# A one-core hybrid layer (SSD, attention, hierarchical MoE): the overflow loop moves from behind the last expert group into the first one

## The chip, the cores and the metric

One NeuronCore of a Trainium2 chip runs the whole program. The metric is the device time of one execution in microseconds (us): 540.91 us is the median of three runs of the kernel before (540.25 to 541.68). Engines are named as in the profile: PE (TensorE matmul) with PEld (its weight loads), DVE (VectorE), ACT (ScalarE), POOL (GpSimd) and SP (SyncE, which here issues all weight loads).

## The reference

```
h   = RMSNorm(x)                          # x: 256 rows of 1024, float32
[z | xBC | dt | q | k | v | g_ssd | g_att] = h @ W_in
y_s = Mamba-2 SSD(z, xBC, dt) @ W_ssd_out
y_a = MoBA(rope(q), rope(k), v) @ W_att_out
x   = x + (sigmoid(g_ssd) * y_s + sigmoid(g_att) * y_a) @ W_o
x   = x + HierMoE(RMSNorm(x))             # top 1 of 4 groups, in it top 2 of 8 experts
gate = sigmoid(RMSNorm(x) @ W_pg)
x   = x + gate * (p @ W_ple)
out = RMSNorm(x)
```

HierMoE is, for each expert e that a row chose, `(silu(x @ w_gate[e]) * (x @ w_up[e])) @ w_down[e]` times the row's weight for e. There are 32 experts with three matrices of 1 MiB each (1024x256, 1024x256 and 256x1024 float32). 256 rows make 512 choices.

## The kernel before

**Stages.** In-projection, SSD, attention and the output projections fill the first 297 us. A middle part of the program then normalizes the new x (in the tile `x_sb`), forms the router's logits (`plg`), chooses experts and ranks the choices of each expert (`choose`, `rank`, `select`, `combine`), and gathers rows for the first experts. The expert stage follows, then a tail: transposes of the sum `y_sb` (`x3_T`), the split of it into a high and a low part (`x3_out`: ACT writes `x3_hi`, DVE `x3_lo`), the same split of the gate matrix W_pg (`gate_hi` on ACT, `gate_lo` on DVE), 3-pass matmuls of both (`ple_gate`), and the last RMSNorm.

**Expert stage.** The function `quad(q)` handles experts 4q to 4q+3. Each expert has 32 slots, so that the four fill 128 rows. The rows are gathered by matmuls with a one-hot matrix (`gat`, evicted into `hTg`); the gate phase multiplies them with the four gate matrices (`gu<-wg`), the up phase with the up matrices (`gu<-wu`), 64 matmul instructions each, as 8 steps of k times 4 experts. `hidden` applies the nonlinearity and transposes (`hq`), `down` makes `py` in two column halves of 512, `ye` is its copy, and `sca` scatters it back to the 256 rows, where DVE adds it into `y_sb`. The group q = 7 is the last: its halves of `py` are scattered each as soon as it is there.

**Overflow.** An expert that was chosen by more than 32 rows has choices left over. `count_rounds` computes how many further rounds that takes (`nov`), and `overflow_rounds` is a loop with that count at run time, `tc.For_i(0, nov, 1)`, which handles up to 8 expert-with-32-slots pieces a round. In the executions here nov is 0: no instruction of the loop's body is in the trace. The loop stands behind the last group, ahead of the tail.

**Order of the loads.** All weights come by SP, one load of 1 MiB into one of 26 pages (8 KB on each of 128 partitions), in the order of the list `queue`: four gate matrices, four up matrices, four down matrices for each group. A load is issued when `prefetch(n)` is reached in the program and a page and one of 8 semaphores of the DMA queue are free; so at most 8 loads are under way. `NPRE = 25` expert loads are asked for ahead of the expert stage, and each phase of a group asks for as many as pages it gave back. The last four down matrices come in halves (`d0`, `d1`), and behind them two of the four pages of W_pg (`pgr`); the other two are asked for behind the loop.

**Order on the engines.** PE, ACT, DVE and POOL follow the written order inside blocks of `manual_schedule` (the middle part and the tail are such blocks) and an order that a scheduler finds elsewhere (the groups 0 to 6). SP always follows the written order. All engines meet at the loop.

Of the kernel before, what the change touches and what calls it, by code (L numbers as in the profile page):

```python
# [15 lines left out]
OP = mybir.AluOpType  # L16
# [166 lines left out]
def emit(ctx, tc, nc, A, out):  # L183
# [8 lines left out]
    def pg(shape, name, dt=F32):  # L192
        return pgp.tile([P] + shape, dt, tag="pg", name=name)
# [622 lines left out]
    def expert_load(e, w):  # L816
        if w[0] == "d":
            if w != "d1":
                EW["d", e] = pg([4, 512], f"wd{e}")
            r = slice(2 * int(w[1]), 2 * int(w[1]) + 2) if w[1:] else slice(0, 4)  # L820
            SP.dma_start(EW["d", e][:, r], A["w_d"][e].rearrange("(p r) d -> p r d", r=4)[:, r])
        else:
            t = pg([NK, 256], f"w{w}{e}")
            SP.dma_start(t, A["w_" + w][e].rearrange("(p k) f -> p k f", k=NK))
            EW[w, e] = t

# [20 lines left out]
    queue = deque((expert_load, 4 * q + j, w) for q in range(NE // 4) for w in "gud" for j in range(4))  # L847
    for _ in range(4):
# [245 lines left out]
    def count_rounds():  # L1094

        pc = ps3([1], "ocount", parts=NE)
        for t in range(NT):
            mm(pc, mk[:, t, :], onesb[:, 0:1], t == 0, t == NT - 1)
        cnt, more, total = tn([1], "ocn0")[0:NE], tn([8], "omore", BF16, 1)[0:NE], tn([1], "ototal", F32, 1)[0:1]
        V.tensor_copy(cnt, pc)  # L1100
        yield
        V.tensor_scalar(more, C("r32")[0:NE], cnt, None, op0=OP.is_lt)
        yield
        pm = ps3([8], "omorep", parts=1)
        mm(pm, onesb[0:NE, 0:1], more, True, True)
        for _ in range(4):
            yield
# [17 lines left out]

    def gather_mm(pgts, t, rhs):
        for k in range(NK):
            mm(pgts[k // 4][:, k % 4, :], x_sb[:, t, k * P:(k + 1) * P], rhs, t + k % 4 == 0, t == NT - 1)
# [66 lines left out]
    middle.__exit__(None, None, None)  # L1195
    for _ in count_rounds():
        pass
    pgts = psos = wrw = None
# [27 lines left out]

    def hidden(pgu, f, n, name, filler=lambda: None):
        hq = qt([512], "hq" + name)
# [4 lines left out]
        filler()  # L1233
        pt = ps2([2, n], "hdT" + name)
# [43 lines left out]

    def quad(q, filler=lambda: None):
        if q:  # L1280
# [6 lines left out]
        for i, w in enumerate("gu"):  # L1287
            if (q, i) == (7, 1):
                sw, f = combine_weights(q, sel)
            for js in GU_ORDER.get((q, i), ((0, 1, 2, 3),)):  # L1290
                for k in range(NK):
                    for j in js:
                        mm(pgu[32 * j:32 * j + 32, 256 * i:256 * i + 256], g(k)[:, 32 * j:32 * j + 32],
                           EW[w, 4 * q + j][:, k, :], k == 0, k == NK - 1)
                for j in js:
                    EW.pop((w, 4 * q + j))
# [6 lines left out]
        hT = hidden(pgu, f, P, str(q), filler)  # L1303
        if q == 7:
# [9 lines left out]
    def overflow_rounds():  # L1314

        nov = nc.values_load(nov_i, min_val=0, max_val=MAXOV - 1,
                             skip_runtime_bounds_check_because="512 choices fill at most 15 rounds beyond the first")
        with tc.For_i(0, nov, 1) as it:
            work = qt([512], "owork")
            pc = ps2([1], "ocnt", parts=NE)  # L1320
# [53 lines left out]
            g = ow = None  # L1374
            sw = weights_T(work[:, 192:192 + NT * CAP], work[:, 256:512], CAP, "o")
            f = factors(lambda t: so[:, t], CAP, "o")
            hT = hidden(pgu, f, CAP, "o")
            for n in range(2):
                s = slice(512 * n, 512 * n + 512)
                py = ps1([512], f"pyo{n}", parts=CAP)  # L1380
                for c in range(2):
# [3 lines left out]
                ow = None  # L1385
                y = qt([512], f"yo{n}")
                SC.copy(y[0:CAP], py)
# [156 lines left out]
    hT = None  # L1544
    gate_hi(0, 0, range(4))
    end.__exit__(None, None, None)
    sw = y = None
# [3 lines left out]
    end.__enter__()  # L1551
# [4 lines left out]
    x3_out(*d10)
# [62 lines left out]
```

## Time and profile before

| | us |
|---|---|
| median of 3 runs | 540.91 (540.25 to 541.68) |
| the profiled execution, its own time | 538.34 |
| its span in the trace | 536.6 |
| PE busy | 497.5 (93%) |
| DVE busy | 287.9 (54%) |
| ACT busy | 212.5 (40%) |
| DMA | 154.77 MB, mean 288 GB/s over the span |

The profiled execution took 1.74 us more than its span and 2.57 us less than the median. Times below are on the axis of that trace (us from the span's start). A chain of waits follows the work that ended last back from the last instruction. A window row gives the busy time of each engine in a stretch, the granted PE clock as a share of 2.4 GHz, the busy share of the DMA engines and what they moved. On DMA rows the landing is the time from the issue by SP to the last byte.

### The profile page before, as it was taken

What the parts mean: (1) busy time and instruction counts of PE and PEld (TensorE: products, weight loads), DVE (VectorE), ACT (ScalarE), POOL (GpSimd) and SP (SyncE); (2) the same over time, 40 slices, a digit from 0 to 9 for tenths busy, and PEclk for the clock granted to TensorE, in tenths of its full rate; (3) what the DMA queues carried; (4) which work ended last, traced back from release to release, by engine and by line L of the source; (5) the groups of instructions that cost most, each with busy time, mean ns of one, the idle gap of its engine ahead of it and who ended that gap; (6) DMA issues with size and microseconds to landing.
All of it is one profiled execution on the core that took longest, in us unless ns stands there. A gap on an engine that the chain in (4) does not pass through costs nothing. (4 is left out here: it accounts for less than half of the span.)

```text
span 536.6 us, 9525 instructions
## 1 busy us (share of the span) xinstructions
PE 497.5 (93%) x3911; PEld 382.6 (71%) x3911; DVE 287.9 (54%) x586; ACT 212.5 (40%) x427; POOL 16.0 (3%) x22
## 2 busy tenths in 40 slices
PE   6999999999999999999999999889898899887793
PEld 3899888798899979999988746355363536352583
DVE  5899788878477595745583612313133220121675
ACT  5927759518375095532352311111111112111473
POOL 3000012000000000000000000000000000000001
PEclk9999999999999999999999989899898999999897
DMA  8990087564627224796689999999999999999402
GB/s 310 426 396 2 1 280 279 165 228 161 233 86 308 79 72 164 288 385 263 257 324 408 360 372 421 419 421 423 417 420 420 415 422 421 418 417 402 177 0 78
DMA packets 29264, 154.77 MB, mean 288 GB/s; under 512 B 4242, under 2 KB 9122, under 8 KB 13348
## 3 DMA queue, kind: packets, MB, share of 16 engines
q1 hardware_dynamic: 29220, 154.16, 72.1%
q8 instruction: 31, 0.51, 0.4%
q14 instruction: 13, 0.11, 0.1%
HBM read 153.08 MB, written 1.06 MB: 287 GB/s over the span
## 5 line engine op out<-in xcount | busy, mean ns | idle before, releaser
L295 DVE TENSOR_TENSOR wl<-wr,wh 128x1024 fp32r<-128x1024 f32 (+4 forms) x92 | 100.8, 1132 | 9.5 <-ACT wh L294 8.6
L294 ACT CAST wh<-wr 128x1024 fp32r<-128x1024 f32 (+4 forms) x92 | 82.6, 961 | 14.5 <-DMA wr<-in_w_ao 4.2
L210 PE MATMUL py<-wd,hq 128*32 128x512 f32 x256 | 37.7, 712 | 3.7 <-ACT hq L1238 3.7
L210 PE MATMUL ps_t<-wl,hT_hi 128*128 128x448 f32 (+2 forms) x112 | 39.9, 373 | 1.2 <-DVE wl L295 1.1
L210 PE MATMUL ps_t<-wh,hT_hi 128*128 128x448 f32 (+2 forms) x112 | 39.6, 375 | 0.0
L210 PE MATMUL ps_t<-wh,hT_lo 128*128 128x448 f32 (+2 forms) x112 | 39.0, 366 | 0.0
L210 PE MATMUL gu<-wu,hTg 128*32 128x256 f32 x512 | 33.0, 379 | 1.8 <-DMA wu<-in_w_u 1.8
L1231 DVE SCALAR_TENSOR_TENSOR hq<-hq,gu 128x256 f32<-128x256 f32 x8 | 3.4, 421 | 55.8 <-ACT hq L1230 55.8
L210 PE MATMUL sca<-ye,selw 128*128 128x512 f32 x64 | 30.2, 612 | 1.5 <-DVE ye L1540 0.8
L210 PE MATMUL gat<-sel,x_sb 128*128 128x128 f32 x256 | 30.3, 276 | 0.5 <-DVE sel L1114 0.5
L210 PEld LDWEIGHTS gat<-sel,x_sb 128*128 128x128 f32 x256 | 29.4, 192 | 1.1 <-DVE sel L1114 0.6
L210 PE MATMUL gu<-wg,hTg 128*32 128x256 f32 x512 | 30.1, 381 | 0.0
L210 PEld LDWEIGHTS py<-wd,hq 128*32 128x32 f32 x256 | 10.2, 126 | 25.6 <-issue 19.2
L210 PEld LDWEIGHTS gu<-wu,hTg 128*32 128x32 f32 x512 | 18.1, 110 | 14.5 <-DMA wu<-in_w_u 2.3
L1311 DVE COPY ye<-py 128x512 f32<-128x512 f32 x7 | 4.8, 692 | 40.3 <-PE py L210 40.3
L210 PEld LDWEIGHTS sca<-ye,selw 128*128 128x128 f32 x64 | 10.9, 189 | 20.4 <-issue 9.1
L210 PEld LDWEIGHTS ps_t<-wl,hT_hi 128*128 128x128 f32 x112 | 21.0, 190 | 4.9 <-DVE wl L295 3.3
L1230 ACT ACTIVATE hq<-gu,f 128x256 f32<-128x256 f32 x8 | 3.8, 474 | 47.7 <-PE gu L210 47.5
L210 PEld LDWEIGHTS ps_t<-wh,hT_lo 128*128 128x128 f32 x112 | 21.3, 190 | 1.9 <-DVE hT_lo L360 0.4
L210 PEld LDWEIGHTS gu<-wg,hTg 128*32 128x32 f32 x512 | 15.4, 110 | 9.9
L210 PEld LDWEIGHTS ps_t<-wh,hT_hi 128*128 128x128 f32 x112 | 21.1, 191 | 1.7
L1137 ACT ACTIVATE hTg<-gat,par 128x128 f32<-128x128 f32 x32 | 9.3, 369 | 27.6 <-PE gat L210 26.2
(310 smaller groups left out, 1100.0 us busy)
## 6 DMA issues: line engine op xcount, KB each, us to landing
wg<-in_w_g SPq DMA_DIRECT2D x32, 1024.0 KB, 13.7
wu<-in_w_u SPq DMA_DIRECT2D x32, 1024.0 KB, 17.4
wd<-in_w_d SPq DMA_DIRECT2D x28, 1024.0 KB, 19.8
wr<-in_w_in SPq DMA_DIRECT2D x16, 1024.0 KB, 5.2
wr<-in_w_in SPq DMA_DIRECT2D x10, 896.0 KB, 10.8
wr<-in_w_so SPq DMA_DIRECT2D x4, 1024.0 KB, 4.7
wr<-in_w_ao SPq DMA_DIRECT2D x4, 1024.0 KB, 7.1
wr<-in_w_o SPq DMA_DIRECT2D x4, 1024.0 KB, 6.9
```

The lines of the kernel that those rows point to most:

```text
L210: mm = lambda o, l, r, start, stop: PE.matmul(o, l, r, start=start, stop=stop, skip_group_check=True)
L294: SC.copy(hi[:, s], raw[:, s])
L295: V.tensor_tensor(lo[:, s], raw[:, s], hi[:, s].bitcast(F32), op=OP.subtract)
L1137: SC.activation(dst(k + i, k + i + 1)[:, 0], o[:, i], AF.Copy, scale=R("mnw")[:, k + i:k + i + 1])
L1230: SC.activation(hd[0:n], pgu[:, 0:256], AF.Tanh, scale=f[0:n, 0:1])
L1231: V.scalar_tensor_tensor(hd[0:n], hd[0:n], 1.0, pgu[:, 0:256], op0=OP.add, op1=OP.mult)
L1311: (V.tensor_copy if c else SC.copy)(y[c], py[c])
```

## The change

The loop with its count is moved; the loads at the end are cut and ordered in another way; the tail is written in another order. `overflow_rounds` gets a page of its own in place of small tiles, and `NPRE` is one less.

```diff
-NPRE = 25
+NPRE = 24
-GU_ORDER = {(7, 1): ((0, 1, 2), (3,))}
...
-    queue.extend((expert_load, NE - 4 + j, w) for w in ("d0", "d1") for j in range(4))
+    queue.extend((expert_load, NE - 4 + j, w) for w in ("u0", "u1", "d0", "d1") for j in range(4))
-    queue.extend((ple_gate_load, kh, c) for kh, c in PG_ORDER[:2])
+    queue.extend((ple_gate_load, kh, c) for kh, c in PG_ORDER)
...
-    gather_mm(pgts, 1, flat(sel, 1))
+    count = count_rounds()
+    next(count), next(count)
+    gather_mm(pgts, 1, flat(sel, 1), range(4))
+    next(count)
+    gather_mm(pgts, 1, flat(sel, 1), range(4, 8))
+    weave(count)
     weave(combine(0))
...
     middle.__exit__(None, None, None)
-    for _ in count_rounds():
-        pass
...
+    def first_sums():
+        ys.append(pg([NT, D], "y_sb"))
+        for t in range(NT):
+            SC.copy(ys[0][:, t], x_sb[:, t])
+
     def scatter(sw, y, n, name):
-        before = ys[0] if ys else x_sb
-        if not ys:
-            ys.append(pg([NT, D], "y_sb"))
...
-                V.tensor_tensor(ys[0][:, t, s], before[:, t, s], po, op=OP.add)
+                V.tensor_tensor(ys[0][:, t, s], ys[0][:, t, s], po, op=OP.add)
...
-                prefetch(len(js) - (q == 0))
+            for j in range(4):
+                EW.pop((w, 4 * q + j))
+            if (q, i) == (0, 0):
+                first_sums()
+                overflow_rounds()
+                prefetch(4)
+            else:
+                prefetch(4 - (q == 0))
...
-    for c in range(2):
-        down(7, c, py, hT)
-        (V.tensor_copy if c else SC.copy)(y[c], py[c])
-        for t in range(NT):
-            scatter7(t, c)
-            add7(t, c)
-    gate_hi(0, 0, range(4))
-    end.__exit__(None, None, None)
-    overflow_rounds()
-    ple_gate_load(*PG_ORDER[2]), ple_gate_load(*PG_ORDER[3])
-    end = tc.manual_schedule(engines={ET.PE, ET.Activation, ET.DVE, ET.Pool})
+    def y7(c):
+        SC.copy(y[c][:, 0:256], py[c][:, 0:256])
+        V.tensor_copy(y[c][:, 256:512], py[c][:, 256:512])
+
+    down(7, 0, py, hT)
+    y7(0)
+    for t in range(NT):
+        scatter7(t, 0)
+        add7(t, 0)
+    down(7, 1, py, hT)
     d00 = x3_T(0, 0)
     d10 = x3_T(1, 0)
+    y7(1)
     x3_out(*d00)
+    gate_hi(0, 0, (0, 1))
+    for t in range(NT):
+        scatter7(t, 1)
+    x3_out(*d10)
+    gate_hi(0, 0, (2, 3))
     gate_lo(0, 0, (0, 1))
-    x3_out(*d10)
+    for t in range(NT):
+        add7(t, 1)
     gate_lo(0, 0, (2, 3))
```

**First place: the first group, PE and SP.** The names: `wu3` is an up matrix, `swT0` the transposed combine weights, `pf` a factor, `nov` the loop's count; before, on PE, from the end of the up phase of group 0:

```order
L210 MATMUL gu0_3245<-wu2_2414,hTg01_3179 32x256
L210 MATMUL gu0_3245<-wu3_2416,hTg01_3179 32x256
L1245 MATMUL swT0_3325<-ident_79,selw0_3322 128x128 x2
L210 MATMUL pf0_3329<-fac_2968,sel0_3145 128x2 x2
L210 MATMUL pf1_3500<-fac_2968,sel1_3386 128x2 x2
```

and now:

```order
L209 MATMUL gu0_3243<-wu2_2414,hTg01_3179 32x256
L209 MATMUL gu0_3243<-wu3_2416,hTg01_3179 32x256
L1324 TENSOR_LOAD nov_2969
L1327 COMPARE_AND_BRANCH
L1327 UNCONDITIONAL_BRANCH x2
```

On PE the loop has come to stand behind the whole up phase of group 0 and ahead of its `swT0`, `pf` and `hdT`. On SP, in the list of loads, before:

```order
L821 DMA wd6_3226<-in_w_d 128x2048
L821 DMA wd7_3228<-in_w_d 128x2048
L824 DMA wg8_3230<-in_w_g 128x2048
L824 DMA wg9_3278<-in_w_g 128x2048
L824 DMA wg10_3280<-in_w_g 128x2048
```

and now (the body of the loop is left out):

```order
L820 DMA wd6_3238<-in_w_d 128x2048
L820 DMA wd7_3240<-in_w_d 128x2048
L1324 TENSOR_LOAD nov_2969
L1327 COMPARE_AND_BRANCH
L1327 UNCONDITIONAL_BRANCH x2
...
L825 DMA wg8_3436<-in_w_g 128x2048
L825 DMA wg9_3438<-in_w_g 128x2048
```

The load of wg8, which was the last of the 25 asked for ahead of the expert stage, and every load after it now stand behind the loop in SP's list.

**Second place: the middle part, ACT and DVE.** `sqm` is the sum of squares of x, `xmTs` the evicted transpose for the logits; on ACT now:

```order
L1005 ACTIVATE sqm11_3096,ssm1_2971<-x_sb_76 128x256
L1012 COPY xmTs14_3111<-xmT14_3108 128x256
L1257 COPY y_sb_3276<-x_sb_76 128x1024
L1005 ACTIVATE sqm12_3120,ssm1_2971<-x_sb_76 128x256
L1257 COPY y_sb_3276<-x_sb_76 128x1024
L1012 COPY xmTs16_3129<-xmT16_3126 128x256
```

The two copies of L1257 are new, and ahead of the last transposes; the other four rows stand in this order before as well. On DVE, in front of and in the chain that makes the expert weights (`ng0` is its first instruction; `omore` and `ototal` belong to the count), before:

```order
L1114 TENSOR_TENSOR sel0_3145<-rk1_2967,cst_74 128x128
L1067 TENSOR_SCALAR ng0_3188<-g80_3066 128x1
L1069 TENSOR_TENSOR dd0_3190<-e80_3073 128x1
L1074 TENSOR_TENSOR el0_3070<-mk_2965,oh10_3099 128x32
...
L1134 TENSOR_TENSOR hTg01_3179<-gat0_1_3164,par_75 128x256
...
L1108 TENSOR_REDUCE ototal_3238<-omorep_3241 1x1
```

and now:

```order
L1113 TENSOR_TENSOR sel1_3545<-rk1_2967,cst_74 128x128
L1102 TENSOR_SCALAR omore_3184<-cst_74,ocn0_3183 32x8
L1107 TENSOR_REDUCE ototal_3185<-omorep_3192 1x1
L1109 CAST nov_2969<-ototal_3185 1x1
L1067 TENSOR_SCALAR ng0_3200<-g80_3066 128x1
```

`ototal` and the cast to `nov`, which stood behind the eviction `hTg01`, have moved ahead of `ng0`; `ototal` reads `omorep`, a matmul that PE now has between the two halves of the gather `gat` of row tile 1.

**Third place: the tail, DVE.** `pgl00` is the low part of the first page of W_pg, `sca7..` what the scatter of the last group makes; before, from the first `x3_lo` on:

```order
L1445 TENSOR_TENSOR x3_lo_4427<-x3T00_4747,x3_hi_4426 128x4x128
L1461 SCALAR_TENSOR_TENSOR pgl00_4574<-pgr00_4366,par_75,pgh00_4573 128x512 x2
L1445 TENSOR_TENSOR x3_lo_4427<-x3T10_4752,x3_hi_4426 128x4x128
L1461 SCALAR_TENSOR_TENSOR pgl00_4574<-pgr00_4366,par_75,pgh00_4573 128x512 x2
L1461 SCALAR_TENSOR_TENSOR pgl01_4766<-pgr01_4406,par_75,pgh01_4765 128x512 x2
```

and now:

```order
L1549 COPY ye71_4709<-py7_1_4707 128x256
L1453 TENSOR_TENSOR x3_lo_4594<-x3T00_4734,x3_hi_4593 128x4x128
L1453 TENSOR_TENSOR x3_lo_4594<-x3T10_4739,x3_hi_4593 128x4x128
L1469 SCALAR_TENSOR_TENSOR pgl00_4749<-pgr00_4567,par_75,pgh00_4748 128x512 x2
L1439 TENSOR_TENSOR y_sb_3276<-y_sb_3276,sca701_0_4752 128x512
L1439 TENSOR_TENSOR y_sb_3276<-y_sb_3276,sca711_0_4754 128x512
L1469 SCALAR_TENSOR_TENSOR pgl00_4749<-pgr00_4567,par_75,pgh00_4748 128x512 x2
```

The last two adds into `y_sb` have moved from ahead of the first `x3_lo` to between the halves of `pgl00`.

## Rows read from the trace of the kernel before

**Rows 1.** Windows of 20 us in the expert stage: busy time (and count) of PE, PEld, DVE, ACT, POOL, then the granted PE clock, the DMA share and GB/s.

```profile
320.00:340.00 20.00, 18.05 (x196) 10.44 (x192) 6.00 (x13) 2.36 (x7) 0.00 (x0) 0.99 1.01 422
...
460.00:480.00 20.00, 17.28 (x171) 9.88 (x160) 5.60 (x11) 2.95 (x8) 0.00 (x0) 1.00 1.01 419
```

**Rows 2.** Timeline of PE, ACT and DVE at the end of the expert stage, up to the loop and the first transposes behind it: start, length, engine, line, instruction, count, and in brackets the idle time before it and what ended it.

```profile
481.29 6.26 PE L210 MATMUL gu<-wu,hTg 128*32 128x256 f32 x60 [1.80 <-DMA wu<-in_w_u]
...
487.63 0.47 ACT L1230 ACTIVATE hq<-gu,f 128x256 f32<-128x256 f32 x1 [8.58 <-PE gu L210]
...
490.09 1.92 PE L210 MATMUL py<-wd,hq 128*32 128x512 f32 x16 [0.46 <-ACT hq L1238]
...
499.40 0.69 DVE L1431 TENSOR_TENSOR y_sb<-y_sb,sca 128x512 f32<-128x512 f32 x1 [0.17 <-PE sca L210]
...
501.23 1.09 PE L1439 MATMUL x3T<-ident,y_sb 128*128 128x128 f32 x8 [1.87 <-DVEq L1318]
```

**Rows 3.** The chain that ended last, in order of time, its first steps: start, length, what ran. "issue" is time in which nothing in the profile was waited for.

```profile
500.36 0.86 issue
501.23 0.67 PE x3T L1439 x4
...
503.28 4.36 PE pgate L210 x11
```

**Rows 4.** The loads of the last two whole up matrices wu30 and wu31, and one of the down halves: issue on SP's queue (first to last), and the time from issue to landing.

```profile
L824 SPq DMA_DIRECT2D wu<-in_w_u x2: 327/328/328, 461.3 to 463.8; - x2
...
DMA to landing us min/median/max: 19.9/19.9/19.9
```

**Rows 5.** SP's timeline of weight loads around the start of the expert stage and in its middle, and of the two pages of W_pg behind the loop: start of the first issue, length, line, what is loaded, count.

```profile
298.16 0.42 SPq L824 DMA_DIRECT2D wg<-in_w_g  x1
...
308.62 0.33 SPq L824 DMA_DIRECT2D wg<-in_w_g  x1
...
372.04 7.82 SPq L821 DMA_DIRECT2D wd<-in_w_d  x4
382.03 7.78 SPq L824 DMA_DIRECT2D wg<-in_w_g  x4
...
500.91 0.89 SPq L842 DMA_DIRECT2D pgr<-in_w_pg  x2
```

**Rows 6.** Timeline of the middle part, PE and ACT, and from the tail the ACT instruction of 128x1024.

```profile
297.11 0.28 PE L210 MATMUL pso1q<-wh,mT 128*128 128x256 f32 x1
...
297.95 0.42 ACT L1005 ACTIVATE sqm<-x_sb 128x256 f32<-128x256 f32 x1 [0.86 <-DVE x_sb L1001]
...
298.50 0.37 ACT L1012 COPY xmTs<-xmT 128x256 f32<-128x256 f32 x1
...
298.28 1.31 PE L210 MATMUL plg<-wrw,xmTs 128*128 128x64 f32 x10
...
514.28 1.04 ACT L1486 ACTIVATE junk<-y_sb 128x1024 f32<-128x1024 f32 x1
```

**Rows 7.** Timeline of the way from the selection to the first group, PE and DVE.

```profile
302.74 0.15 DVE L1067 TENSOR_SCALAR ng<-g 128x1 f32<-128x1 f32 x1
302.87 2.05 PE L210 MATMUL gat<-sel,x_sb 128*128 128x128 f32 x16 [0.50 <-DVE sel L1114]
...
304.12 0.42 DVE L1134 TENSOR_TENSOR hTg<-gat,par 128x256 f32<-128x256 f32 x1
...
304.94 3.66 PE L210 MATMUL gu<-wg,hTg 128*32 128x256 f32 x64
308.42 3.64 PE L210 MATMUL gu<-wu,hTg 128*32 128x256 f32 x64
```

**Rows 8.** Windows of 2 us: the highest rate near the start of the expert stage, and the stretch in which the loads ran out (columns as in rows 1).

```profile
294.00:296.00 2.00, 2.00 (x20) 2.00 (x18) 1.83 (x11) 0.40 (x1) 0.00 (x0) 1.00 1.06 446
...
306.00:308.00 2.00, 2.00 (x45) 1.18 (x38) 1.07 (x7) 0.41 (x4) 0.00 (x0) 1.00 0.69 279
308.00:310.00 2.00, 2.00 (x44) 1.23 (x40) 0.00 (x0) 0.00 (x0) 0.00 (x0) 1.00 0.34 78
310.00:312.00 2.00, 2.00 (x41) 0.99 (x33) 0.00 (x0) 0.00 (x0) 0.00 (x0) 1.00 0.87 340
```

**Rows 9.** Timeline of the tail: ACT's high parts of a page of W_pg, DVE's low part of x and of W_pg, and PE's first matmul of the second row tile.

```profile
502.88 2.57 ACT L1454 ACTIVATE pgh<-pgr,par 128x512 fp32r<-128x512 f32 x4
...
508.12 0.59 ACT L1444 CAST x_hi<-x3T 128x512 fp32r<-128x512 f32 x1 [2.67 <-PE x3T L1439]
...
502.54 0.69 DVE L1445 TENSOR_TENSOR x_lo<-x3T,x_hi 128x512 fp32r<-128x512 f32 x1 [2.45 <-ACT x_hi L1444]
...
505.07 2.73 DVE L1461 SCALAR_TENSOR_TENSOR pgl<-pgr,par,pgh 128x512 fp32r<-128x512 f32 x4
...
507.49 0.60 PE L1439 MATMUL x3T<-ident,y_sb 128*128 128x128 f32 x4
507.84 0.48 PE L210 MATMUL pgate<-pgh,x_hi 128*128 128x512 f32 x1
```

**Rows 10.** Windows of the loop's crossing, of the first part of the tail and of the rest of its matmuls (columns as in rows 1).

```profile
499.40:501.20 1.80, 0.00 (x0) 0.00 (x0) 0.68 (x1) 0.00 (x0) 0.00 (x0) 1.00 0.04 14
503.30:506.70 3.40, 3.40 (x8) 2.72 (x9) 3.40 (x6) 2.15 (x4) 0.00 (x0) 0.50 1.01 424
507.80:527.90 20.10, 20.10 (x115) 17.48 (x113) 14.94 (x27) 12.42 (x23) 2.03 (x3) 1.00 0.00 0
```

More of the change, by code (lines that the diff above doesn't have):

```diff
@@ L822, in expert_load @@
         else:
-            t = pg([NK, 256], f"w{w}{e}")
-            SP.dma_start(t, A["w_" + w][e].rearrange("(p k) f -> p k f", k=NK))
-            EW[w, e] = t
+            if w[1:] != "1":
+                EW[w[0], e] = pg([NK, 256], f"w{w[0]}{e}")
+            r = slice(4 * int(w[1]), 4 * int(w[1]) + 4) if w[1:] else slice(0, NK)
+            SP.dma_start(EW[w[0], e][:, r], A["w_" + w[0]][e].rearrange("(p k) f -> p k f", k=NK)[:, r])
     def ple_load():
@@ L847, in emit @@
     queue = deque((expert_load, 4 * q + j, w) for q in range(NE // 4) for w in "gud" for j in range(4))
-    for _ in range(4):
+    for _ in range(8):
         queue.pop()
-    queue.extend((expert_load, NE - 4 + j, w) for w in ("d0", "d1") for j in range(4))
+    queue.extend((expert_load, NE - 4 + j, w) for w in ("u0", "u1", "d0", "d1") for j in range(4))
     queue.insert(PLE_AT, (ple_load,))
     queue.insert(PLE_AT, (rows_load,))
-    queue.extend((ple_gate_load, kh, c) for kh, c in PG_ORDER[:2])
+    queue.extend((ple_gate_load, kh, c) for kh, c in PG_ORDER)
     def prefetch(n):
@@ L1105, in count_rounds @@
         mm(pm, onesb[0:NE, 0:1], more, True, True)
-        for _ in range(4):
-            yield
+        yield
         V.tensor_reduce(total, pm, axis=AX.X, op=OP.add)
@@ L1124, in gather_tiles, with gather_mm @@
         return [a[:, 0:4 * n].rearrange("p (k n) -> p k n", k=4) for a in acc("gat" + name)]
-    def gather_mm(pgts, t, rhs):
-        for k in range(NK):
+    def gather_mm(pgts, t, rhs, ks=range(NK)):
+        for k in ks:
             mm(pgts[k // 4][:, k % 4, :], x_sb[:, t, k * P:(k + 1) * P], rhs, t + k % 4 == 0, t == NT - 1)
@@ L1195, in emit @@
     middle.__exit__(None, None, None)
-    for _ in count_rounds():
-        pass
+    count = None
     pgts = psos = wrw = None
@@ L1225, in factors, with hidden @@
         return f
-    def hidden(pgu, f, n, name, filler=lambda: None):
-        hq = qt([512], "hq" + name)
+    def hidden(pgu, f, n, name, hq=None):
+        hq = qt([512], "hq" + name) if hq is None else hq
         hd = hq[:, 0:256]
@@ L1277, in down, with quad @@
                 EW.pop(("d", 4 * q + j))
-    def quad(q, filler=lambda: None):
+    def quad(q):
         if q:
@@ L1289, in quad @@
                 sw, f = combine_weights(q, sel)
[L1290 to L1296, printed above, removed]
-                prefetch(len(js) - (q == 0))
+            for k in range(NK):
+                for j in range(4):
+                    mm(pgu[32 * j:32 * j + 32, 256 * i:256 * i + 256], g(k)[:, 32 * j:32 * j + 32],
+                       EW[w, 4 * q + j][:, k, :], k == 0, k == NK - 1)
+            for j in range(4):
+                EW.pop((w, 4 * q + j))
[5 more added lines that the diff above has]
+                prefetch(4 - (q == 0))
         if q == 0:
@@ L1302, in quad @@
             sw, f = combine_weights(q, sel)
-        hT = hidden(pgu, f, P, str(q), filler)
+        hT = hidden(pgu, f, P, str(q))
         if q == 7:
@@ L1317, in overflow_rounds @@
                              skip_runtime_bounds_check_because="512 choices fill at most 15 rounds beyond the first")
+        page = pg([4, 512], "opage")
         with tc.For_i(0, nov, 1) as it:
-            work = qt([512], "owork")
+            work, hq, y = (page[:, i] for i in range(3))
+            g = page[:, 3, 0:256].rearrange("p (k c) -> p k c", k=NK)
             pc = ps2([1], "ocnt", parts=NE)
@@ L1373, in overflow_rounds @@
                         mm(pgu[:, 256 * i:256 * i + 256], g[:, k2 + k, :], ow[:, k, :], k2 + k == 0, k2 + k == NK - 1)
-            g = ow = None
+            ow = None
             sw = weights_T(work[:, 192:192 + NT * CAP], work[:, 256:512], CAP, "o")
             f = factors(lambda t: so[:, t], CAP, "o")
-            hT = hidden(pgu, f, CAP, "o")
+            hT = hidden(pgu, f, CAP, "o", hq)
             for n in range(2):
                 s = slice(512 * n, 512 * n + 512)
-                py = ps1([512], f"pyo{n}", parts=CAP)
+                py = acc(f"pyo{n}", 1)[0][0:CAP]
                 for c in range(2):
@@ L1385, in overflow_rounds @@
                 ow = None
-                y = qt([512], f"yo{n}")
                 SC.copy(y[0:CAP], py)
@@ L1537, in emit @@
     y = [qt([512], f"ye7{c}") for c in range(2)]
[L1538 to L1551 removed]
+    def y7(c):
[7 more added lines that the diff above has]
+    down(7, 1, py, hT)
     d00 = x3_T(0, 0)
     d10 = x3_T(1, 0)
+    y7(1)
     x3_out(*d00)
+    gate_hi(0, 0, (0, 1))
[3 more added lines that the diff above has]
+    gate_hi(0, 0, (2, 3))
     gate_lo(0, 0, (0, 1))
[L1556 removed]
+    for t in range(NT):
+        add7(t, 1)
     gate_lo(0, 0, (2, 3))
+    hT = sw = y = py = None
     gate_hi(0, 1, range(4))
```

4 lines of the change are left out of this document (1 added, 3 removed).

## The prediction, made before the changed kernel ran

> **What bounds the kernel now.** I read the summary first (PE busy 93%, DMA 288 GB/s on average), then the windows, because an average says nothing on a kernel with stages. At 320 and still at 460 us the DMA share is 1.0 and about 420 GB/s arrive, with PE busy about 90% [rows 1]. PE is nearly full, but what it waits for in the last group shows who leads: its up phase stands 1.80 us for a matrix that has just landed [rows 2]. wu31, the last, was issued at 463.8 and landed 19.9 us later, at 483.7 [rows 4]; eight loads of 2.5 us each are under way (four issues in 9.99 us, [rows 5]). So the end of the expert stage is set by the stream, and the stream by the moment from which it ran without a gap. That moment is the start of the first group: 8 loads are not asked for before pages come back, and from 306 to 310 the rate falls to 279 and 78 GB/s; it is back at 340 GB/s in 310 to 312 [rows 8]. SP issues wg8 at 298.16 and the next load only at 308.62, when the gate phase (304.94 to 308.60) has given its pages back [rows 5, 7].
>
> Behind the last load the chain of waits counts [rows 3]: rest of the up phase, tanh at 487.63, `py` at 490.09, scatter, last add to 500.09, crossing of the loop, transposes at 501.23, `pgate` of row tile 1 at 507.84 [rows 2, 9], and from there PE is busy in every microsecond up to 527.9 at full clock with no DMA left [rows 10]. So I follow two numbers through the change: T, the landing of the last up matrix (483.7), and G, the start of `pgate` of row tile 1 (507.8). Behind G both programs have the same work in the same order, which I cost at nothing.
>
> **The change part by part.**
>
> *The y_sb copies.* Two ACT copies of 128x1024 now stand ahead of the last `xmTs`. The nearest row of that size takes 1.04 us [rows 6]. The first lies mostly in the 0.86 us for which ACT was idle at 297.1 to 297.95, and pushes `sqm` by about 0.4; the second delays `xmTs` by all of its length, so `xmTs` ends near 300.1 in place of 298.87, and the last logits with it: +1.2 [rows 6]. Bounds: 0, if the x that they copy is not what ACT waits for and they slip in earlier; 2.1, both in full.
>
> *The count in the middle.* On DVE `ototal` waits for `omorep`, which PE has after half of a gather that takes 2.05 us. With the 1.2 us above, the gather starts at 304.07, its half ends at 305.1, `omorep` (bounded by a matmul of that gather, about 0.16) at 305.25, and two tiny DVE instructions (0.15 like `ng`) let `ng` start at 305.6. From `ng` to the end of `hTg` were 1.80 us (302.74 to 304.54), so the gate phase starts at 307.4, not 304.94: +2.5 in all [rows 7]. Bounds: 1.2, if `ng` is not held, and 3.5.
>
> *The loop in group 0.* Its body doesn't run, but it is a place where all engines meet. By its order PE gets there behind the whole up phase, not between gate and up phase as the source reads: 307.4 + 7.12 (304.94 to 312.06) = 314.55. SP came out of the loop 0.82 us after the last add (500.09 to 500.91) and PE 1.14 after it [rows 2, 3, 5]. So SP issues again at 315.4, where it did at 308.62: +6.8. Meanwhile nothing is under way, since all 24 loads in front of the loop have long landed. At the old place the crossing costs nothing any more: -1.14 behind the last add.
>
> *NPRE 24.* One load more lies behind the gap: +2.5 [rows 5].
>
> Both sums meet at the stream. It is full from the gap to the end, so nothing gives them back: T = 483.7 + 6.8 + 2.5 = 493.0. Lower bound: with no delay of the gate phase the issue is at 312.9, T + 6.8. The gap itself can't be below: the order leaves nothing to issue. What PE has to do behind the loop comes 4 us late too, but groups 6 and 7 wait for their loads anyway.
>
> *Halves of the up matrices.* When the last half lands, 19 of the 32 steps are done (k 0 to 3 of all, and three of k 4), 13 remain: 13/32 of 3.64 us, 1.5, and some filling, 1.7. The up phase ends at 494.7. Before it ended at 487.55, 3.85 after its last load [rows 2]. Gain 2.1. The hidden part keeps its 2.5 us (487.55 to 490.09): `hq` is ready at 497.2.
>
> *Down halves.* They come behind T at 1.25 us each: d0 of expert 31 at 498.0, d1 at 503.0. This is a wait that the earlier T had hidden as well, but with nothing to spare now: the second half of `py` can't end before 503.0 plus its last five of eight steps (three fifths of 1.92 and the pipeline, 1.7) = 504.7.
>
> *The tail's order.* The transposes of the first column half (8 in 1.09 us) follow at once, to 505.8, the first four to 505.3. The first page of W_pg lands 2.5 us behind the last d1, at 505.5, the others at 508.0, 510.5 and 513.0. ACT: `x_hi` (0.59) to 505.9, two rows of `pgh` (0.64 each) to 507.2, `x_hi` to 507.8. DVE, in its order: `x_lo` of row tile 1 to 508.5, two `pgl` (0.68 each) to 509.9, two adds (0.69 each) to 511.3, two `pgl` to 512.7. The last matmuls of `pgate` of row tile 0 end 0.3 later, four transposes (0.45) follow, and G = 513.45 [rows 2, 9]. Before, from T to G were 24.1 us; now they are 20.45. The tail gains 3.7 and the stream loses 9.3: +5.6.
>
> A half clock of PE (0.50, 1.2 GHz) stood in 503.3 to 506.7, right behind PE's idle stretch at the loop: 8 matmuls in 3.4 us, which are 1.7 at the full level [rows 10]. In my sum that place is set by DVE and pays nothing. If the new idle time at 510 brings the half clock behind G, it costs up to 1.7 more. The Trainium skill (TensorE: Matmul & The Clock Gate, "What's actually happening") says that the array falls to 1.2 GHz when it has been idle and comes back with activity; the 0.50 row agrees, and by that rule the time would be up to 1.7 us above the forecast.
>
> In the profiled execution's terms the sum is 538.34 + 5.6 = 543.9; that execution lies 2.57 under the median, so the forecast is 540.91 + 5.6 = 546.5. Its own range goes from +3.1 (lower bound of T, 6.8 - 3.7) to +7.5 (bound of the gate phase 3.5 in place of 2.5, half of the clock).
>
> **Rivals.**
>
> *The stream makes the gap up (faster).* 72.6 MB (some 69 loads) lie behind the gap. At 420 GB/s they take 172.9 us, at 446, the highest window [rows 8], 162.8: 10 us back, more than the 9.3 lost. Then T is 483.0, and only the tail's 3.7 and 0.7 are left: 536.5. For it: PE is busy 90%, so PE and the stream are nearly level, and the queue starts empty and full of pages. Against: the stream started from such a gap before too, and then stayed at 419 to 422 in windows of 20 us [rows 1]; the 446 is one window of 2 us, with transfers of another shape.
>
> *It makes up about half (no change).* 433 GB/s give back 5.2 us of the 9.3, and with the tail's 3.7 that is +0.4: 541.3. The same rows speak for and against. The Trainium skill (DMA: Bandwidth & Descriptors, "Specifications") gives 435 GB/s as the ceiling of the fabric; the 420 of the trace is close under it, and one 2 us window of 446 is over it. By that ceiling alone the stream could give back 6.0 us, and the time would be about 540.5.
>
> *The change is costlier than the sum (slower by more).* Twelve loads at 2.5 make 30 us for a group, and with PE busy about 90% [rows 1] its work fills some 27 of them. If PE, which starts group 2 with an empty stream and waits for each load in turn, falls to the half clock in those waits (0.50 was seen, [rows 10]), each microsecond there adds half a microsecond of work. From 6 us at half clock in a group on, the slack of 3 us is used up, PE becomes the bound and holds back pages. One group with 12 such us costs 3 us: 549.5. Against: the two windows of rows 1, with PE at 86 to 90%, have clocks of 0.99 and 1.00.
>
> *The loop is passed early.* If SP did not need to meet PE at the loop, SP would issue at 308.6 + 2.5 and the loss would be 2.5 + 2.5 - 3.7 = +1.3: 542.2. Against: at its old place SP did wait, to 0.82 us after the last add.
>
> **How the numbers follow.** Forecast with its own range 0.67; the worse case 0.10; loop passed early 0.05; half made up 0.06; all made up 0.12. Less than 0.3% (1.6 us) can't be told from no change in a measurement of this kernel. Faster by more: 0.12, and 0.04 for a part of the half case and for what I have not seen, 0.16. Within: 0.06. Slower: 0.78. The range 541.0 to 550.0 holds the forecast, the worse case, the early loop and a part of the half case.
>
> **What would show it.** In the profile of the changed kernel: SP's issue of wg8 near 315.4 and no landing between about 308 and 317; gate phase of group 0 from 307.4; PE idle for about 1.1 us at the end of group 0's up phase; the last half of an up matrix landing at 493; `hq` of group 7 at 497; G at 513.5, with DVE's two adds between `pgl` rows in front of it; no loop at 500. I am wrong if the last up half lands before 487, or if the stretch from it to G is not within 2 us of 20.5.

## The result, and the profile after

The changed kernel takes 547.40 us (median of 4 runs, 544.61 to 549.12) where the kernel before takes 540.58 (4 runs): ratio 1.0121, 95% interval 1.0073 to 1.0169. It is slower by 6.8 us, 3.9 to 9.1 by the interval. The forecast was 546.5 us, +5.6.

The profiled execution of after has a span of 542.8 us (before 536.6). Of these 6.2 us, 0.48 lie ahead of everything that was changed: the last `pso1q` matmul starts at 297.59, and at 297.11 before [rows 6]. From there on the traces differ by 5.7 us. Since this start varies from execution to execution (297.1 to 301.4 in the traces below), times are counted from it where two kernels are compared.

The timeline of after from the middle part to the start of the stream, ACT, DVE, PE and SP:

```profile
297.59 0.28 PE L209 MATMUL pso1q<-wh,mT 128*128 128x256 f32 x1
297.91 1.05 ACT L1257 COPY y_sb<-x_sb 128x1024 f32<-128x1024 f32 x1 [0.35 <-PE pso1q L209]
299.27 1.03 ACT L1257 COPY y_sb<-x_sb 128x1024 f32<-128x1024 f32 x1
300.21 0.36 ACT L1012 COPY xmTs<-xmT 128x256 f32<-128x256 f32 x1
...
305.85 0.15 DVE L1107 TENSOR_REDUCE ototal<-omorep 1x1 f32<-1x8 f32 x1 [0.94 <-PE omorep L209]
...
307.95 3.66 PE L209 MATMUL gu<-wg,hTg 128*32 128x256 f32 x64 [1.06 <-DVE hTg L1133]
311.43 3.64 PE L209 MATMUL gu<-wu,hTg 128*32 128x256 f32 x64
...
315.43 2.94 SPq L825 DMA_DIRECT2D wg<-in_w_g  x4
```

The two copies stand ahead of the last `xmTs`, DVE waits 0.94 us for `omorep`, and the gate phase begins 10.36 us after the last `pso1q`; before it was 7.83 [rows 6, 7]. PE runs gate and up phase in one go, to 315.07, and only then, at 315.43, SP issues wg8. The windows show what that does to the stream (columns as in rows 1):

```profile
312.00:314.00 2.00, 2.00 (x44) 1.17 (x36) 0.00 (x0) 0.00 (x0) 0.00 (x0) 1.00 0.00 0
314.00:316.00 2.00, 1.07 (x20) 0.39 (x12) 0.20 (x1) 0.00 (x0) 0.00 (x0) 1.00 0.00 0
316.00:318.00 2.00, 1.19 (x9) 0.97 (x9) 0.83 (x5) 0.35 (x1) 0.00 (x0) 1.00 0.84 184
318.00:320.00 2.00, 1.23 (x9) 0.90 (x8) 1.11 (x5) 0.70 (x3) 0.00 (x0) 1.00 1.02 426
320.00:340.00 20.00, 19.89 (x200) 10.66 (x204) 4.93 (x10) 2.16 (x7) 0.00 (x0) 0.91 1.01 423
...
420.00:440.00 20.00, 16.53 (x180) 9.30 (x182) 2.99 (x7) 2.36 (x7) 0.00 (x0) 0.91 1.01 415
440.00:460.00 20.00, 18.84 (x52) 7.45 (x45) 3.85 (x7) 4.03 (x7) 0.00 (x0) 0.83 1.02 423
460.00:480.00 20.00, 17.74 (x203) 10.32 (x202) 3.15 (x6) 3.43 (x9) 0.00 (x0) 1.00 1.01 419
```

From 312 to 316 nothing moves at all. From 318 on the stream is as full as before: the windows of 20 us from 320 to 480 have 415 to 423 GB/s, and 416 to 422 before. Nothing of the gap is given back. The chain that ended last, which before did not go back beyond the tail, now begins at the loop (315.20), follows PE through the first groups up to 371.56, and from there runs along the loads into the tail (some of its steps, in order of time):

```profile
371.56 19.81 DMA wu<-in_w_u
...
467.95 17.71 DMA wu<-in_w_u
485.72 10.29 DMA wd<-in_w_d
496.08 10.67 DMA pgr<-in_w_pg
506.75 1.31 ACT pgh L1462 x2
```

The last link is not to be taken at its word: `pgh` starts at 506.73 directly behind `x_hi` on ACT (rows below), and its page, issued at 494.80, had landed 11.4 us later, at 506.2. What leads to `pgh` is the last up half, the second half of `py`, `x3T` and `x_hi`.

The end of the expert stage and the tail of after (before: [rows 2, 9]):

```profile
493.49 1.91 PE L209 MATMUL gu<-wu,hTg 128*32 128x256 f32 x26 [0.78 <-DMA wu<-in_w_u]
...
495.49 0.47 ACT L1233 ACTIVATE hq<-gu,f 128x256 f32<-128x256 f32 x1 [6.00 <-PE gu L209]
...
497.95 2.56 PE L209 MATMUL py<-wd,hq 128*32 128x512 f32 x16 [0.46 <-ACT hq L1240]
...
501.43 1.98 PE L209 MATMUL sca<-ye,selw 128*128 128x512 f32 x4 [0.92 <-DVE ye L1549]
...
503.35 2.28 PE L209 MATMUL py<-wd,hq 128*32 128x512 f32 x16
...
505.56 1.09 PE L1447 MATMUL x3T<-ident,y_sb 128*128 128x128 f32 x8
...
506.25 0.58 ACT L1452 CAST x_hi<-x3T 128x512 fp32r<-128x512 f32 x1 [0.21 <-PE x3T L1447]
506.73 1.33 ACT L1462 ACTIVATE pgh<-pgr,par 128x512 fp32r<-128x512 f32 x2
...
510.50 1.27 DVE L1439 TENSOR_TENSOR y_sb<-y_sb,sca 128x512 f32<-128x512 f32 x2
...
513.49 0.60 PE L1447 MATMUL x3T<-ident,y_sb 128*128 128x128 f32 x4
513.85 0.48 PE L209 MATMUL pgate<-pgh,x_hi 128*128 128x512 f32 x1
```

PE's last wait for an up half ends at 493.49, with 26 instructions left (13 steps of two). `pgate` of row tile 1 starts 20.4 us later, at 513.85.

### The profile page after: what moved, and what is told of

Read it like the earlier page. It is cut to its first block, busy times and chain, and to the rows that moved or that the text cites. A ratio compares the mean times of both kernels' runs of the same rounds, so it can differ in the third digit from the quotient of the medians.

```text
span 542.8 us, 9535 instructions
## 1 busy us (share of the span) xinstructions
PE 500.2 (92%) x3911; PEld 381.4 (70%) x3911; DVE 288.4 (53%) x587; ACT 214.0 (39%) x430; POOL 15.8 (3%) x22
## 5 line engine op out<-in xcount | busy, mean ns | idle before, releaser
L209 PE MATMUL py<-wd,hq 128*32 128x512 f32 x256 | 41.3, 727 | 3.7 <-ACT hq L1240 3.7
L209 PE MATMUL gu<-wu,hTg 128*32 128x256 f32 x512 | 31.6, 380 | 2.5 <-DMA wu<-in_w_u 2.5
L209 PEld LDWEIGHTS gu<-wu,hTg 128*32 128x32 f32 x512 | 17.0, 110 | 14.9 <-DMA wu<-in_w_u 4.0
L1264 DVE TENSOR_TENSOR y_sb<-y_sb,sca 128x512 f32<-128x512 f32 x28 | 19.2, 687 | 4.6 <-PE sca L209 4.6
```

What stands on the lines that cost most here:

```text
L209: mm = lambda o, l, r, start, stop: PE.matmul(o, l, r, start=start, stop=stop, skip_group_check=True)
L1264: V.tensor_tensor(ys[0][:, t, s], ys[0][:, t, s], po, op=OP.add)
```

## The experiments

All times below marked "after `pso1q`" are counted from the start of the last `pso1q` matmul of the same trace. "Last up wait" is the end of PE's last wait for an up load. The kernel before waits last for its second to last matrix (184.18), and its last one lands at 186.59 [rows 2, 4].

| | gate phase | SP issues behind the gap | last up wait | ratio (95%) |
|---|---|---|---|---|
| before | 7.83 | 11.51 | 184.18 (landing 186.59) | |
| after | 10.36 | 17.84 | 195.90 | 1.0121 (1.0073 to 1.0169) |
| e3, no loop | 10.36 | 14.03 | 191.95 | 1.0004 (0.9964 to 1.0044) |
| e4, loop behind the gate phase | 11.08 | 15.13 | 193.29 | 1.0060 (1.0030 to 1.0090) |
| e5, copies and count moved | 8.02 | 15.50 | 193.46 | 1.0073 (1.0038 to 1.0107) |
| e8, e4 and e5 together | 8.02 | 12.07 | 189.88 | 0.9998 (0.9966 to 1.0031) |
| e12, before, one page held | 7.83 | 11.50 | 186.70 | 1.0039 (1.0011 to 1.0068) |
| e2, end parts alone | 7.83 | 11.50 | 186.92 | 0.9921 (0.9891 to 0.9952) |

The delays add up. The up halves end their last wait at 186.92 in e2, whose stream starts as before. To this add what SP's issue came later than 11.50, and 2.52 for the one load more that lies behind the gap (e12 against before). That gives 195.78 for after, 191.97 for e3, 193.07 for e4, 193.44 for e5 and 190.01 for e8; each measured value is within 0.25 us of it.

### The stream: e3, e4, e5, e8

**e3** takes the loop out of the first group and leaves everything else:

```diff
                 first_sums()
-                overflow_rounds()
                 prefetch(4)
```

> The whole change without the overflow loop (its rounds are left out). Theory (the loop in group 0 is what delays the loads): wg8 is issued when the gate phase ends, near 311.6 instead of 315.4, and the last up half lands 4 to 5 us earlier than in the change, near 489; time +1.3 to +2.0 us over before, ratio 1.003. Rival (the copies, the count and 24 loads cost it all, or the stream gives the gap back): the time stays at that of the change, ratio 1.010 or more.

Measured: 541.42 us, ratio 1.0004. The timeline of e3, PE and SP:

```profile
297.83 0.28 PE L209 MATMUL pso1q<-wh,mT 128*128 128x256 f32 x1
...
311.86 2.07 SPq L825 DMA_DIRECT2D wg<-in_w_g  x4
...
489.78 1.91 PE L209 MATMUL gu<-wu,hTg 128*32 128x256 f32 x26 [0.65 <-DMA wu<-in_w_u]
```

wg8 is issued 3.8 us earlier after `pso1q` than in after, and the last up wait ends 3.95 us earlier: the stream passes on what SP lost, one for one. The rival (a ratio of 1.010 or more) is outside the interval. The time is below what was expected (1.003), which its interval still holds. wg8 is issued only when the gate phase ends (308.19 + 3.66), although no loop stands in its way: that is the page which `y_sb` holds (e12 below).

**e4** lets PE meet the loop where the source has it. The loop's body loads its weights through the four quarter tiles; two of these hold the gathered rows of group 0 until the up phase has read them. The body gets a second page, which is free at that place, and PE the written order:

```diff
+        if q == 0:
+            first = tc.manual_schedule(engines={ET.PE})
+            first.__enter__()
         for i, w in enumerate("gu"):
...
+            first.__exit__(None, None, None)
...
+        page2 = pg([4, 512], "opage2")
...
-                    ow = qt([2, 256], f"o{w}{k2}")
+                    ow = page2[:, k2 // 2].rearrange("p (a b) -> p a b", a=2)
...
-                    ow = qt([512], f"owd{n}{c}")
+                    ow = page2[:, 2 * n + c]
```

> The change, with the loop's body loading into a second page of its own instead of the quarter tiles that hold the first group's gathered rows, and PE in the written order, so that PE meets the loop right behind the gate phase and not behind the up phase. Theory (SP waits in the loop for PE's up phase): SP issues wg8 near 312.5 in place of 315.4, everything behind comes 3 us earlier, +3 us over before, ratio 1.006. Rival (the loop's own crossing or the drained stream is the cost, wherever PE meets it): as the change, ratio 1.011 to 1.013.

Measured: 544.26 us, ratio 1.0060. The timeline of e4, PE and SP:

```profile
310.38 3.66 PE L209 MATMUL gu<-wg,hTg 128*32 128x256 f32 x64 [1.05 <-DVE hTg L1133]
315.74 3.66 PE L209 MATMUL gu<-wu,hTg 128*32 128x256 f32 x64 [1.71 <-issue]
...
314.43 2.69 SPq L825 DMA_DIRECT2D wg<-in_w_g  x4
```

PE stands 1.71 us between gate and up phase, and SP issues 0.4 us after the gate phase's end (310.38 + 3.66). After `pso1q` that is 2.7 us earlier than in after, and the last up wait 2.6 us. So it is PE's place at the loop that sets the gap. (In this execution the gate phase itself came 0.7 us later, behind a gather at half clock.)

**e5** puts the two copies behind the last `xmTs` on ACT, and `ototal` and `nov` behind the eviction of `hTg` on DVE, and leaves the loop where the change has it:

```diff
+    first_sums()
     rank(1)
     select(sel, 0, 1)
...
-    weave(count)
     weave(combine(0))
...
+    weave(count)
     hTg[0] = (lambda k: hT0[k // 4][:, k % 4]), sel
...
-                first_sums()
                 overflow_rounds()
```

> The change with the two y_sb copies behind the last evicted transposes on ACT, and ototal and nov behind the eviction of hTg on DVE; the loop stays behind group 0's up phase. Theory (these two delay the gate phase by 2.5 us, and the full stream passes that on): the gate phase starts 7.8 us after the last pso1q matmul as before, not 10.4, and the time falls by 2.5 us against the change: ratio to before 1.007 to 1.008. Rival (the loop hides it): no shift, ratio 1.012.

Measured: 543.52 us, ratio 1.0073. The gate phase starts 8.02 us after `pso1q` in place of 10.36, SP and the last up wait follow by 2.3 and 2.4 us. The two delays are real, and paid in full.

**e8** joins both:

> e4 and e5 together: the loop directly behind the gate phase, copies and count out of the way. Theory (each place costs what it holds up in the stream): gate phase at the time of before, SP's next issue 0.5 us behind its end, one load more behind the gap 2.5, the end of the program 3.5 faster: -0.5 us against before, ratio 0.999. Rival (a loop inside the first group drains the queue and costs in itself): ratio 1.005 or above.

Measured: 541.15 us, ratio 0.9998, which is what was expected and excludes the rival. A loop in the first group, placed there, costs the stream little in itself: SP issues 0.56 us later than before (12.07 against 11.51).

### The load more behind the gap: e9, e12

**e9** is the kernel before with one edit:

```diff
-NPRE = 25
+NPRE = 24
```

> The kernel before with 24 in place of 25 loads asked for ahead of the expert stage, and nothing else. Theory (from the first gap on the stream is full, so a load that falls behind the gap is paid in full): the last up matrix lands 2.5 us later against the gate phase, ratio 1.004 to 1.005. Rival (the queue refills with more loads at once and gives it back): ratio 1.000 to 1.002.

Measured: 541.04 us, ratio 0.9978 (0.9947 to 1.0009), and the last up wait 184.18 after `pso1q`, the same as before. A miss: the edit moves nothing, so it puts no load behind the gap and doesn't try the theory. The load wg8 is now asked for by the gate phase's own `prefetch`, but one page is free and SP runs ahead of PE, so it is issued at the same place as before. What holds it back in the change is the page that `y_sb` takes early, and the loop in SP's list.

**e12** therefore takes the page as well:

```diff
-NPRE = 25
+NPRE = 24
...
+    held = [pg([NT, D], "y_sb")]
+    G.memset(held[0][0:1, 0, 0:1], 0.0)
     prefetch(NPRE - nload[0])
...
-            ys.append(pg([NT, D], "y_sb"))
+            ys.append(held.pop())
```

> The kernel before with 24 loads ahead and the page of y_sb taken (by writing one number into it) ahead of them, as in the change, so that wg8 really has to wait for a page of the gate phase; in e9 a page was free and wg8 was issued early all the same. Theory (a load behind the gap is paid in full by the full stream): wg8 is issued at the end of the gate phase, the last up matrix lands 2.5 to 2.8 us later against the last pso1q matmul, ratio 1.004 to 1.006. Rival (four loads asked for at once refill the queue and give it back): last up matrix within 1 us of before, ratio 0.999 to 1.002.

Measured: 543.84 us, ratio 1.0039 (1.0011 to 1.0068). The timeline of e12, the last `pso1q`, SP, and the last group's up phase on PE:

```profile
297.62 0.28 PE L210 MATMUL pso1q<-wh,mT 128*128 128x256 f32 x1
...
309.12 2.09 SPq L824 DMA_DIRECT2D wg<-in_w_g  x4
...
484.32 7.95 PE L210 MATMUL gu<-wu,hTg 128*32 128x256 f32 x60 [1.72 <-DMA wu<-in_w_u]
```

wg8 is issued with wg9, 11.50 after `pso1q`, and the last up wait ends 2.52 us later than before (186.70 against 184.18): the price of one load, 2.5, as in the sum. The rival had that time within 1 us of before; the ratio alone, whose interval begins at 1.0011, would not exclude it.

### The end: e2, e11, e1, e6

**e2** keeps only the end of the change: up halves, four pages of W_pg behind the down loads, the new tail. It has no overflow loop, and count and sums stand where they stood before.

```diff
-NPRE = 24
+NPRE = 25
...
-            if (q, i) == (0, 0):
-                first_sums()
-                overflow_rounds()
-                prefetch(4)
-            else:
-                prefetch(4 - (q == 0))
+            prefetch(4 - (q == 0))
```

> Only the end of the change (up halves, four gate pages behind the down loads, the new tail), no overflow loop anywhere (its rounds are left out), 25 loads ahead, count and sums as before. Theory: the last up half lands at 483.7 as before, pgate of row tile 1 starts 20.5 us later near 504.2, 3.7 us faster than before, ratio 0.993. Rival (smaller loads or the longer queue slow the stream): the last up half lands 1.5 us or more later, and the time is within 1 us of before or above it.

Measured: 537.02 us, ratio 0.9921 (0.9891 to 0.9952), the gain as worked out. The last up half is there 0.3 us after the time at which the last matrix of before lands, so the halves don't slow the stream. **e11** is e2 with the last up matrices whole, in the order of before:

```diff
-    queue.extend((expert_load, NE - 4 + j, w) for w in ("u0", "u1", "d0", "d1") for j in range(4))
+    queue.extend((expert_load, NE - 4 + j, w) for w in ("d0", "d1") for j in range(4))
...
+            for js in (((0, 1, 2), (3,)) if (q, i) == (7, 1) else ((0, 1, 2, 3),)):
```

> As e2 (end of the change alone, no loop anywhere, overflow rounds left out), but with the last up matrices whole and multiplied in the order of before (three experts, then the fourth). Theory (the halves bring hq 1.6 to 2.1 us forward, of which the down halves' landing leaves about 1 us): 1 us slower than e2, ratio 0.993 to 0.995. Rival (the halves carry the whole gain of the end parts): ratio 0.998 or more; other rival (nothing, the down halves set the end): as e2, 0.992.

Measured: 538.93 us, ratio 0.9948 (0.9916 to 0.9979). It lies where the theory puts it, between the rivals, but its interval overlaps that of e2, so that the halves carry about a third of the gain is likely and not settled.

**e1** is the kernel before without its loop:

```diff
     sw = y = None
-    overflow_rounds()
     ple_gate_load(*PG_ORDER[2]), ple_gate_load(*PG_ORDER[3])
```

> The kernel before without its overflow loop (the rounds beyond the first are left out; with these inputs there are none). Theory (the loop at its old place costs its crossing and no more): the first transposes start 0.2 us after the last add in place of 1.14, so about 1 us faster than before, ratio 0.998. Rival (the half clock behind the loop is a consequence of the loop's idle time): the half-clock stretch goes too, another 1.7 us, 2.7 us in all, ratio 0.995.

Measured: 538.47 us, ratio 0.9975 (0.9947 to 1.0002): about 1.4 us, near what the crossing alone would give; the rival's 0.995 is just inside the interval. The trace speaks for the rival's mechanism and not for its price. Around and behind the last add the clock is full (1.00 from 500 to 507), while in all five traces with the loop there (before, e7, e9, e10, e12) a stretch of 0.50 follows it. But the first half of `py` now runs at half clock (0.50 from 490.2 to 493.6) and takes 3.50 us, where before it took 1.92 [rows 2]. Up to `pgate` of row tile 1 the trace gains 0.1 us.

```profile
490.37 3.50 PE L210 MATMUL py<-wd,hq 128*32 128x512 f32 x16 [0.46 <-ACT hq L1238]
```

**e6** moves the loop alone, with loads and tail of the end as before:

> Only the first half of the change: loop, count and copies in group 0, 24 loads ahead; the last up matrices whole, and the tail in the order of before (without the loop there). Theory (costs add): last up matrix landing 9.3 us later than before, the old loop's crossing of about 1 us gone: +8.3 us, ratio 1.014 to 1.017. Rival (a later stream is hidden by the old tail's slack, so the two halves of the change don't add): ratio 1.010 or less.

Measured: 546.75 us, ratio 1.0116 (1.0079 to 1.0153). This decides nothing: the interval reaches from the rival to the theory. In its trace the last up matrix lands at 493.0, 9.0 us later than before after `pso1q`. But the edit left out, as the change does, the order of three experts before the fourth, which the whole matrices would have needed, and PE did a part of that up phase at half clock. The trace ends 10.2 us later than before after `pso1q`, the median only 5.7: the traced execution lies above the median of e6 (548.89 against 546.75), that of before below its own (538.34 against 540.58).

### A loop with loads under way: e7, e10

**e7** was meant to take the gain of the end without its order: the kernel before, loop at its old place, with up halves and all four pages of W_pg queued ahead of the loop.

```diff
-    queue.extend((ple_gate_load, kh, c) for kh, c in PG_ORDER[:2])
+    queue.extend((ple_gate_load, kh, c) for kh, c in PG_ORDER)
...
     overflow_rounds()
-    ple_gate_load(*PG_ORDER[2]), ple_gate_load(*PG_ORDER[3])
```

> The kernel before with only the loads of the end changed: up halves, all four gate pages behind the down loads; the loop stays where it was, ahead of the tail. Theory: hq is ready 1.6 us earlier, but the down halves then set the last add, about 1 us earlier than before: ratio 0.997 to 0.999. Rival (the gain is in the tail's order alone): 1.000 or above.

Measured: 543.61 us, ratio 1.0061 (1.0031 to 1.0091): slower, and not for the rival's reason, as its trace shows. The timeline of e7, SP's issue of the four pages and the way from the last add to the first transposes, and windows of the same stretch (columns as in rows 1):

```profile
486.61 4.16 SPq L843 DMA_DIRECT2D pgr<-in_w_pg  x4
...
500.25 0.69 DVE L1432 TENSOR_TENSOR y_sb<-y_sb,sca 128x512 f32<-128x512 f32 x1 [0.17 <-PE sca L210]
506.41 1.97 PE L1440 MATMUL x3T<-ident,y_sb 128*128 128x128 f32 x8 [6.20 <-SPq L1319]
```

```profile
500.00:502.00 2.00, 0.21 (x1) 0.00 (x0) 0.77 (x2) 0.61 (x2) 0.00 (x0) 1.00 0.94 393
502.00:504.00 2.00, 0.00 (x0) 0.00 (x0) 0.00 (x0) 0.00 (x0) 0.00 (x0) 1.00 0.46 188
504.00:506.00 2.00, 0.00 (x0) 0.00 (x0) 0.00 (x0) 0.00 (x0) 0.00 (x0) 0.68 0.09 37
```

PE waits 6.20 us for SP, until the DMA has run dry. SP itself was done with issuing the four pages at 490.8, so it isn't the issue that is waited for: the crossing waits for the landing of every load in front of it. If that is so, **e10**, which differs from e7 only in that two of the pages stand behind the loop again, must lose the wait:

> As e7 (the kernel before, loop at its old place, up halves), but with two pages of W_pg ahead of the loop and two behind it, as before. Theory (the loop waits until all loads in front of it have landed; in e7 the third and fourth page held it up by 6 us): PE's wait at the loop falls to 1.9 us or less as before, ratio 0.997 to 0.999. Rival (the halves or the order of k made e7 slow): ratio 1.004 to 1.006 as e7.

The first row behind the loop in the timeline of e10:

```profile
502.01 1.09 PE L1440 MATMUL x3T<-ident,y_sb 128*128 128x128 f32 x8 [1.93 <-DVEq L1319]
```

The wait is 1.93 us, as before (1.87, [rows 2]), and the time 539.35 us, ratio 0.9961 (0.9931 to 0.9992). e10 keeps the overflow rounds and is faster than before by 0.4%, and so than after. In its one trace the gain doesn't show (span 537.1): its first half of `py` ran 4.15 us in place of 2.56 in e2.

## Why the prediction was right

- **The copies**, +1.2: the last `xmTs` starts 2.62 us after `pso1q` where it was 1.39, +1.23.
- **The count**, +2.5 together with the copies: the gate phase +2.53; e5 gives 2.34 of it back by order alone.
- **The loop in group 0**, +6.8 to SP's issue: +6.33 after `pso1q` (17.84 against 11.51). The crossing was mis-sized: SP was out 0.36 us after PE's last matmul, not 0.82 as at the old place. PE stood 1.75 us there and not 1.1; the DMA share of 1.01 and more from 318 on shows that the stream did not wait for it. That PE passes the loop behind the up phase, read from the order alone, is shown by e4, and so is the price of that.
- **One load behind the gap**, +2.5: e12 +2.52. The size is right and the named cause is not: e9 shows that `NPRE` 24 alone moves nothing, and e12 that the page which `y_sb` takes early is needed.
- **T**, 493.0, +9.3: 493.49 on the trace's axis, +9.3 after `pso1q` (195.90 against 186.59). That it fits to a tenth is in part luck: 6.33 and 2.52 make 8.85, and 0.33 is what e2's last wait for a half ends behind the landing of before's last whole matrix, which the sum didn't have.
- **The halves**, up phase ended 1.7 us after T: tanh starts 2.0 us after it, 3.9 before.
- **Down halves**: I let the landing of the last d1 set the end of the second half of `py` (504.7). In the trace it begins at 503.35, directly behind the scatter of the first half, has its weight load wait for a down half up to 503.72 (the last one, issued at 493.46, takes 10.3 us, to 503.7), and ends at 505.63. So the landing does set the end, 0.7 us later than forecast, with 1.9 us of work behind it in place of 1.7. That term was 0.9 us too small; less of it reached G, because DVE's and ACT's rows behind it fitted more tightly.
- **G**: 513.85 against 513.45 forecast. From T to G 20.36 us against 20.45.
- **Behind G**, costed at nothing: 28.95 us to the end of the span against 28.76.

The profiled executions differ by 6.3 us and the medians by 6.8. Both traced executions lie below their medians, by 2.2 us (before) and 2.8 (after), and three things differ from trace to trace. The first is the start of the last `pso1q` (297.1 to 301.4). The second is the place that the forecast's own upper part named: the half clock behind G, up to 1.7. The trace of after has none there, but other kernels with the same tail do. From the second to the third group of transposes are 3.2 us in after, e3 and e11, and 4.6 to 4.8 in e2, e4, e5 and e8. The window of e4:

```profile
513.90:518.70 4.80, 4.80 (x18) 3.80 (x17) 2.94 (x5) 0.59 (x1) 0.00 (x0) 0.64 0.00 0
```

In the traces with the old tail and its loop (before, e7, e9, e10, e12) the same step takes 3.2 us every time; the half clock lies ahead of it there [rows 10]. PE had been idle for DVE just ahead of this step. The Trainium skill (TensorE: Matmul & The Clock Gate, "What's actually happening") has the array fall to 1.2 GHz after idle time, with which the 0.64, a mean of both levels, agrees; but after, e3 and e11 have the same idle time there (1.36, 1.36 and 1.35 us) and keep the full clock, so that idle time alone doesn't settle it.

The third is `py`. Its first half takes 2.56 us in after, and 4.0 to 4.2 in e3, e4, e8 and e10. From PE's last wait for an up half to the end of the span are 49.3 us in after, and 49.7 to 52.2 in e2, e3, e4, e5 and e8, which have the same end. The old end varies as well. e9, whose loads move as before, runs parts of its last up phase and of `py` at half clock (0.50 from 485.1 to 488.4 and from 495.3 to 498.7):

```profile
485.06 7.92 PE L210 MATMUL gu<-wu,hTg 128*32 128x256 f32 x60 [1.71 <-DMA wu<-in_w_u]
...
495.53 3.47 PE L210 MATMUL py<-wd,hq 128*32 128x512 f32 x16 [0.46 <-ACT hq L1238]
```

In before these are 6.26 and 1.92 [rows 2], and from the last wait on e9 takes 57.9 us to the end where before takes 55.3. So neither trace stands for its median, and what makes up the 0.5 us between 6.3 and 6.8, which is far inside the interval, stays open.

Of the rivals, "the stream makes the gap up" fell by 415 to 423 GB/s in the windows of 20 us, "the loop is passed early" by SP's issue behind PE's up phase, and "costlier than the sum" did not occur: in every window of 20 us from 320 to 500 the DMA share is 1.01 to 1.03, so the stream never ran dry, although PE's clock fell to 0.83 in one of them. Two things that the forecast held against its rivals were misread. The clocks of 0.99 and 1.00 in rows 1 are not typical: other windows of before have 0.91 and 0.93. And the 446 GB/s are not of transfers of another shape: 109 of the 125 packets of that window are of 8 KB or more, like the 8 KB that a load brings each partition. Windows as short as 2 us scatter: before's own stream has one of 438, inside a window of 20 us with 422 [rows 1]:

```profile
322.00:324.00 2.00, 2.00 (x6) 0.80 (x6) 1.61 (x4) 0.00 (x0) 0.00 (x0) 1.00 1.04 438
```

The Trainium skill (DMA: Bandwidth & Descriptors, "Specifications") puts the ceiling of the fabric at 435 GB/s, by which, as an estimate, 6.0 us of the gap could have come back; the same page ("Where 436 GB/s comes from") lets the memory side bind such loads at some 358. The trace lies between, at 415 to 423, and nothing came back.

## What to carry to other kernels

Where one stream of loads is full from its first gap to the end, as here, everything that lengthens the gap is paid in full, microsecond for microsecond, however idle the engine is on which it stands. A loop with a run-time count cost here, even with no rounds, a meeting of the engines and the landing of every load in front of it: put it where the slowest engine has just arrived and no load is under way, and see by the order on each engine where it really stands, not by the source. Of the kernels with rounds e10, with the loop at its old place, has the lowest ratio (0.9961); that of e8 (0.9998) overlaps it. A number that limits loads, such as NPRE, moves nothing as long as a page is free.

## What the runs showed that was not expected

- The crossing of the loop waits for all loads in front of it: 6.20 us of PE's wait in e7 with two more pages queued, 1.93 in e10. In the change this costs nothing, as all 24 loads had landed before (0 GB/s from 312 to 316).
- The crossing itself took SP 0.36 us in after and PE 1.71 us in e4, against 0.82 and 1.14 at the old place.
- Executions of the kernel before spread from 538.29 to 545.68 us over 29 runs, wider than the three runs shown at first. Ten runs of e1 against these 29 leave an interval of 1.5 us to either side, so that an effect of 1 us is not settled by them.
